# A one-core transformer trunk with a mixture of experts: new places for the gather buffers, three weight loads issued later, and a hand-written order for GpSimd's tail

## The chip, the cores and the metric

The kernel runs on one core of one Trainium2 chip. Its engines are TensorE (PE in the rows; PEld is its loading of weights), VectorE (DVE), ScalarE (ACT), GpSimd (POOL) and SyncE (SP, which here only issues DMAs). The metric is the device time of one execution in microseconds.

## The reference

```python
def reference(x, ...):
    h = x
    for l in range(DEPTH):                       # DEPTH = 1, SEQ = 1024 tokens, D_MODEL = 1024
        h = h + hybrid_mixer(rms_norm(h, norm1_g[l]), ...)      # mLSTM heads ++ gMLP groups, W_out
        h = h + hierarchical_moe(rms_norm(h, norm2_g[l]), ...)  # 32 experts, top 2
    return rms_norm(h, final_g)

def hierarchical_moe(xn, w_rg, b_rg, w_re, b_re, w_gate, w_up, w_down):
    ...                                          # a group of experts, then the top 2 of its 8 experts
    def expert_block(args):                      # 128 rows of tokens that chose expert e
        xblk, e = args
        hid = jax.nn.silu(xblk @ w_gate[e]) * (xblk @ w_up[e])      # 1024 -> 512
        return hid @ w_down[e]                                       # 512 -> 1024
    ...                                          # each row weighted and added to its token
```

## The kernel before

The first 470 us or so are the mixer, in two halves of 512 tokens. The last thing that it does (`last_out`) is the second half of the output projection, one tile of 128 tokens at a time; behind each tile stand its normalisation for the experts (`scaled`, `logits_c`, `normed`, which writes the normed tokens to `xd` in DRAM) and its routing: `route_a` (which two experts), `route_pr`, `route_so`, `route_c` (the slot of each token at its experts) and `route_d` (GpSimd scatters token and weight to the table `slots`). The products of matrices take three passes of TensorE: an operand is split by ScalarE and VectorE into a rounded part `wr` and a rest `wl` (`split`, L106 and L107), and `mm3` (L111 to L113) multiplies the parts.

Then `ranks()` orders the 32 experts by their number of tokens: matmuls over `masks`, a short chain on VectorE (`key`, `kc`, `rk`, `ohp`), the matmul of L913 and the list `perm`, from which SyncE and GpSimd read the numbers of the experts. The first three experts (NSTAT = 3) are fixed ones; their tokens' numbers come from `toki` (L873). After `ranks()` the pools of the mixer are closed and the pool `mo` is opened on their memory:

```python
    rk = ranks()
    stA.close()
    mo = ctx.enter_context(tc.tile_pool(name="mo", bufs=2, side="right"))
    xes = [mo.tile([P, D], F32, name=f"xe{i}", bufs=1) for i in range(NXE)]
```

Three tiles `xe0` to `xe2` take the gathered tokens of the next experts. `fetch` reads an expert's slots (`sx_`) and gathers its tokens from `xd` by an indirect DMA of GpSimd (L1042). For each expert, TensorE transposes the tokens (L1102, `prep`), ScalarE and VectorE split them (`split_ps`, L1048 and L1049), then come the products with gate and up (each with its weights in four chunks of 512 KB), `hid` = silu(gate) * up (L1146), its transposes (L1153, `turn`), and the product with down; the result is added to `hd` in DRAM by an indirect DMA. The transposes of `hid` of one expert stand in TensorE's order in the middle of the next expert's gate product. Experts with few tokens (64 rows or less) are multiplied without splitting, by L1056.

The weights come in chunks of 512 KB into a cycle of 35 buffers (`slot`, `wchunk`), nearly all issued by SyncE, in the order of their use. A buffer is free when its chunk has been split, or multiplied. The chunks of the first experts are loaded during the mixer (`prefetch`, `prefetch_first`); `held` are the first PD = 3 chunks of the third expert's down matrix. Before, they are issued by ScalarE at the end of `last_out`.

The order of each engine's instructions is the tile framework's own up to the second expert of the loop, but for `last_out`, where all engines keep the program's order; from the second expert on TensorE, VectorE and ScalarE keep the program's order (`by_hand`).

The tail: eight tiles of 128 finished rows come back from `hd`. `stage_a` sums the squares on ScalarE and takes the root by a pow on GpSimd (L1335); `stage_b` multiplies on VectorE (L1345) and stores (SyncE, L1346). The last expert's rows are added apart (`rows_sum`), written back to `hd` (L1358), normalised (`rows_a`, `rows_b`) and scattered to the output (L1350), after all stores. In the tail VectorE and ScalarE keep the program's order (TMS); GpSimd's is the framework's.

## Time and profile before

| | |
|---|---|
| time, median of 3 runs | 1079.59 us (1076.97 to 1082.15) |
| the profiled execution's own time | 1077.55 us |
| its span, from the first to the last instruction | 1075.8 us |
| TensorE busy | 984.6 us, 92% |
| VectorE, ScalarE, GpSimd busy | 600.1, 520.9, 207.9 us |
| mean DMA rate over the span | 262 GB/s |

All times of rows are microseconds from the start of the span. The profiled execution's own time is 1.8 us more than its span, and 2.0 us less than the median of the three runs. A tile's name in a row stands without its number; `out<-in` is what an instruction writes and reads.

### The profile page before, as it was taken

How to read it: one execution, taken by the hardware profiler on the slowest of the kernel's cores; microseconds unless marked ns; L12 is line 12 of the kernel's file. 1: busy time of each engine (PE TensorE's matmuls, PEld its weight loads, DVE VectorE, ACT ScalarE, POOL GpSimd, SP SyncE). 2: the span in 40 equal slices, each digit the busy share in tenths (PEclk: the TensorE clock that was granted, in tenths of full speed). 3: DMA queues.
4: the chain of work that ended last, by engine and by line, in shares of the span. 5: the costliest groups of instructions: out<-in, count | busy, mean ns of one | idle time of the engine just before them, and what ended most of it. 6: DMA issues, size and time to landing. Idle time of an engine off the chain costs nothing. (4 is left out here: it accounts for less than half of the span.)

```text
span 1075.8 us, 16181 instructions
## 1 busy us (share of the span) xinstructions
PE 984.6 (92%) x5489; PEld 762.7 (71%) x5489; DVE 600.1 (56%) x1234; ACT 520.9 (48%) x779; POOL 207.9 (19%) x259
## 2 busy tenths in 40 slices
PE   6999999999999999949999999999799998999960
PEld 6999887889899887737766666655566665767520
DVE  6644899656655897677834342433342455658123
ACT  6753645255534553347834433444333464758222
POOL 4310000011300000343212222321211221311123
PEclk9999999999999999979999999999899998999995
DMA  7534212444239313976999999999999999999985
GB/s 273 183 99 124 80 67 72 144 136 132 80 105 351 99 60 107 344 271 210 366 330 396 373 362 372 347 377 389 363 381 364 356 364 374 354 373 392 389 313 221
DMA packets 105460, 282.28 MB, mean 262 GB/s; under 512 B 13666, under 2 KB 40370, under 8 KB 105376
## 3 DMA queue, kind: packets, MB, share of 16 engines
q1 hardware_dynamic: 92080, 251.76, 63.8%
q0 software_dynamic: 11712, 24.75, 8.9%
q10 hardware_dynamic: 1584, 4.72, 1.2%
q8 instruction: 44, 0.72, 0.3%
q14 instruction: 40, 0.33, 0.1%
HBM read 261.62 MB, written 25.72 MB: 267 GB/s over the span
## 5 line engine op out<-in xcount | busy, mean ns | idle before, releaser
L107 DVE TENSOR_TENSOR wl<-raw,wr 128x1024 fp32r<-128x1024 f32 (+2 forms) x219 | 259.1, 1191 | 195.8 <-ACT wr L106 183.1
L106 ACT ACTIVATE wr<-raw 128x1024 fp32r<-128x1024 f32 (+2 forms) x219 | 223.6, 1028 | 229.7 <-PE acc L113 166.4
L111 PE MATMUL acc<-wr,r 128*128 128x512 f32 (+2 forms) x688 | 265.1, 386 | 1.7 <-ACT r L1048 0.9
L112 PE MATMUL acc<-wl,r 128*128 128x512 f32 (+2 forms) x688 | 260.5, 379 | 0.0
L113 PE MATMUL acc<-wr,l 128*128 128x512 f32 (+2 forms) x560 | 208.3, 375 | 0.0
L111 PEld LDWEIGHTS acc<-wr,r 128*128 128x128 f32 x688 | 130.5, 190 | 25.5 <-issue 5.1
L112 PEld LDWEIGHTS acc<-wl,r 128*128 128x128 f32 x688 | 130.8, 190 | 15.2 <-issue 0.5
L1056 PE MATMUL acc<-raw,r 128*64 128x256 f32 (+1 forms) x864 | 132.3, 453 | 2.6 <-ACT r L1083 2.4
L113 PEld LDWEIGHTS acc<-wr,l 128*128 128x128 f32 x560 | 106.2, 190 | 11.4 <-DVE l L235 0.6
L1056 PEld LDWEIGHTS acc<-raw,r 128*64 128x64 f32 x864 | 59.8, 138 | 58.8 <-issue 27.9
L111 PE MATMUL acc<-wr,xer 128*128 128x512 f32 x144 | 59.9, 416 | 0.0
L113 PE MATMUL acc<-wr,xel 128*128 128x512 f32 x144 | 57.4, 398 | 0.0
L112 PE MATMUL acc<-wl,xer 128*128 128x512 f32 x144 | 57.3, 398 | 0.0
L1102 PEld LDWEIGHTS sm<-ident,xe 64*128 64x128 f32 (+1 forms) x272 | 33.9, 197 | 31.8 <-issue 15.8
L1056 PE MATMUL acc<-raw,xer 128*64 128x256 f32 x448 | 52.9, 383 | 0.7 <-ACT xer L1083 0.7
L1102 PE MATMUL sm<-ident,xe 64*128 64x64 f32 (+1 forms) x272 | 38.8, 286 | 14.9 <-DMA xe<-xd,toki 8.6
L111 PE MATMUL acc<-r,wr 128*128 128x512 f32 x128 | 51.5, 402 | 0.0
L112 PE MATMUL acc<-l,wr 128*128 128x512 f32 x128 | 51.0, 398 | 0.0
L113 PE MATMUL acc<-wr,r 128*128 128x512 f32 x128 | 50.7, 396 | 0.0
L113 PE MATMUL acc<-r,wl 128*128 128x512 f32 x128 | 50.5, 395 | 0.0
L1056 PEld LDWEIGHTS acc<-raw,xer 128*64 128x64 f32 x448 | 30.8, 137 | 17.3 <-issue 1.0
L1083 ACT ACTIVATE r<-sm 128x256 f32<-128x256 f32 (+1 forms) x28 | 12.7, 453 | 44.4 <-PE sm L1153 44.1
(477 smaller groups left out, 1368.9 us busy)
## 6 DMA issues: line engine op xcount, KB each, us to landing
raw<-in_w_up_dram SPq DMA_DIRECT2D x119, 512.0 KB, 11.6
raw<-in_w_down_dram SPq DMA_DIRECT2D x113, 512.0 KB, 11.2
raw<-in_w_gate_dram SPq DMA_DIRECT2D x111, 512.0 KB, 11.6
raw<-in_w_in_dram SPq DMA_DIRECT2D x24, 412.0 KB, 3.5
raw<-in_w_in_dram SPq DMA_DIRECT2D x16, 512.0 KB, 3.9
raw<-in_w_out_dram SPq DMA_DIRECT2D x16, 512.0 KB, 3.6
raw<-in_w_in_dram SPq DMA_DIRECT2D x16, 410.0 KB, 4.0
l<-in_w_gate_dram SPq DMA_DIRECT2D x11, 512.0 KB, 12.8
```

What stands on the lines that cost most here:

```text
L106: nc.scalar.activation(r[:, :n], raw[:, :n], AF.Copy)
L107: nc.vector.tensor_tensor(l[:, :n], raw[:, :n], r[:, :n].bitcast(F32), op=OP.subtract)
L111: nc.tensor.matmul(ps, ar, br, start=first, stop=False)
L112: nc.tensor.matmul(ps, ar, bl, start=False, stop=False)
L113: nc.tensor.matmul(ps, al, br, start=False, stop=last)
L1056: nc.tensor.matmul(ps[q * H:(q + 1) * H, :n], x, w[:, q * n:(q + 1) * n], start=first, stop=last)
L1083: nc.scalar.activation(x, ps[0][:, :kt * H], AF.Copy)
L1102: nc.tensor.transpose(ps[-1][:, k % per * w:(k % per + 1) * w], xk_[:w, k], ident[:w, :w])
```

## The change

Four edits. The pool `mo` first makes five tiles (`spare`), so that `xe0` to `xe2` lie 16 KB further up: before, `xe0` lay on the last flips' buffers `kT` and `qT`, and `xe1` on `key` and `ohp`; after, all three lie on the mixer's `y` (and the end of `xe2` on `lga`), while the split tokens `xer` and `xel` lie where `xe0` and `xe1` did. The first gather is made at once there, and the last tile's two scatters (`route_d`) stand behind it instead of ahead of it in the text. The three chunks `held` are issued by ScalarE behind the first expert's split tokens (`pin["XE"]`). In `last_out` the last multiply of `scaled` moves from VectorE to GpSimd. In the tail GpSimd too keeps the program's order, and the write-back of the last rows becomes a step of its own, next to last.

```diff
--- before.py
+++ after.py
@@ -43,7 +43,7 @@
 LOOK = 8
 YS = (5, 7)
 E_ = mybir.EngineType
-TMS = (E_.DVE, E_.Activation)
+TMS = (E_.DVE, E_.Activation, E_.Pool)
 MS = (E_.PE, E_.DVE, E_.Activation, E_.Pool)
 NXE = 3
 RE, RL, RT = 14, 9, 3
@@ -664,8 +664,6 @@
                 with tc.issue_after(pin["POOL"].ins):
                     route_d(T // P - 2, 0)
                     route_d(T // P - 2, 1)
-                    route_d(T // P - 1, 0)
-                    route_d(T // P - 1, 1)
                 break
             if nh:
                 po = [acc() for _ in range(TT)]
@@ -782,12 +780,10 @@
             if t + 1 == TT:
                 prefetch_first()
             prefetch(XO + RE + RL + PF[t])
-        scaled(g0 + TT - 1, ys[TT - 1], 1, nc.vector)
+        scaled(g0 + TT - 1, ys[TT - 1], 1)
         raw_logits(g0 + TT - 1, 1)
         normed(TT - 1)
         prefetch(XO + RE + RL + PF[-1], eng=nc.scalar)
-        for z in sources(NSTAT - 1, 2)[:PD]:
-            held.append(wchunk(z, nc.scalar, True))
         route_d(g0 + TT - 3, 1)
         route_a(g0 + TT - 1)
         route_pr(g0 + TT - 1)
@@ -1021,11 +1017,30 @@
     rk = ranks()
     stA.close()
     mo = ctx.enter_context(tc.tile_pool(name="mo", bufs=2, side="right"))
+    spare = [mo.tile([P, KT, P], F32R, name="xe" + q, bufs=1) for q in "rl"]
+    spare += [mo.tile([P, FF], F32, name="hid", bufs=2) for _ in range(2)]
+    spare.append(mo.tile([P, D], F32, name="yo", bufs=1))
     xes = [mo.tile([P, D], F32, name=f"xe{i}", bufs=1) for i in range(NXE)]
     for a in xes[NSTAT:]:
         nc.scalar.activation(a, nhalf[:, 0:1].to_broadcast([P, D]), AF.Copy)
     slots5 = slots.rearrange("(b e) w -> b e w", e=NE)
     ngat = [0]
+
+    gathered = {}
+
+    def gather(at, n, a=None):
+        if a is None:
+            a = xes[ngat[0] % NXE]
+            ngat[0] += 1
+        pin["XG"] = nc.gpsimd.indirect_dma_start(out=a[:n], out_offset=None, in_=xd,
+                                                 in_offset=bass.IndirectOffsetOnAxis(ap=at, axis=0),
+                                                 bounds_check=T - 1, oob_is_err=False)
+        return a
+
+    gathered[0] = gather(toki[:, 0:1], P)
+    with tc.issue_after(pin["XG"].ins):
+        route_d(T // P - 1, 0)
+        route_d(T // P - 1, 1)
 
     def fetch(e, base, n, a=None):
         sx_ = mo.tile([P, 1, 4], I32, name="sx_", bufs=8)
@@ -1036,16 +1051,14 @@
             rows_ = slots5[base:base + n] if isinstance(base, int) else slots5[ds(base, n)]
             nc.gpsimd.dma_start(sx_[:n], rows_[:, ds(e, 1)])
         if a is None:
-            a = xes[ngat[0] % NXE]
-            ngat[0] += 1
-        at = toki[:n, e:e + 1] if isinstance(e, int) else sx_[:n, 0, 0:1]
-        nc.gpsimd.indirect_dma_start(out=a[:n], out_offset=None, in_=xd,
-                                     in_offset=bass.IndirectOffsetOnAxis(ap=at, axis=0),
-                                     bounds_check=T - 1, oob_is_err=False)
+            a = gathered.pop(e) if isinstance(e, int) and e in gathered else \
+                gather(toki[:n, e:e + 1] if isinstance(e, int) else sx_[:n, 0, 0:1], n)
+        else:
+            gather(sx_[:n, 0, 0:1], n, a)
         return a, sx_, n
 
     def split_ps(ps, r, l):
-        nc.scalar.activation(r, ps, AF.Copy)
+        pin["XE"] = nc.scalar.activation(r, ps, AF.Copy)
         nc.vector.tensor_tensor(l, ps, r.bitcast(F32), op=OP.subtract)
 
     H = P // 2
@@ -1265,9 +1278,12 @@
         last = i + 1 == NE
         if i == 0:
             ahead()
-            feed()
             cur = Expert(blks[r], take, pump)
             cur.prep()
+            with tc.issue_after(pin["XE"].ins):
+                for z in sources(NSTAT - 1, 2)[:PD]:
+                    held.append(wchunk(z, nc.scalar))
+            feed()
         while loads and loads[0][0] <= i + 1:
             j, e, m = loads.pop(0)
             skip[0] = (e, m) == (NE - 1, 2)
@@ -1355,6 +1371,8 @@
         for nh in range(2):
             hv, pd = slice(nh * 512, (nh + 1) * 512), prev.pd[0][nh]
             nc.vector.tensor_tensor(rows_[:n, hv], rows_[:n, hv], pd[:n], op=OP.add)
+
+    def rows_back():
         nc.gpsimd.indirect_dma_start(out=hd, out_offset=bass.IndirectOffsetOnAxis(ap=sx[:n, 0, 1:2], axis=0),
                                      in_=rows_[:n], in_offset=None, bounds_check=T + P - 1, oob_is_err=True)
 
@@ -1370,7 +1388,7 @@
             steps.append((stage_a, t))
         if t:
             steps.append((stage_b, t - 1))
-    steps.append((rows_b,))
+    steps += [(rows_back,), (rows_b,)]
     for f, at in ((rows_a, YS[1]), (rows_sum, YS[0])):
         steps.insert(at, (f,))
     with tc.manual_schedule(engines=set(TMS)):
```

**VectorE at the end of the routing.** The rows behind the token numbers `toki`; `key` to `ohp` is the ranking, `ws` to `idxs` the last tile's slots, `wl` the splits of the first expert's gate matrix. Before:

```order
L905 SCALAR_TENSOR_TENSOR key<-sm,keyr 32x32
L907 SCALAR_TENSOR_TENSOR kc<-sm,keyc 32x1
L909 TENSOR_SCALAR key<-key,kc 32x32
L910 TENSOR_REDUCE rk<-key 32x1
L912 TENSOR_SCALAR ohp<-row_304,rk 32x32
L914 CAST perm<-sm 1x32
L916 COPY cnt<-sm 48x32
L875 SCALAR_TENSOR_TENSOR ws<-d,sg 128x1
L877 RECIPROCAL pay<-ws 128x1
L878 TENSOR_TENSOR pay<-d,pay 128x1
L880 SCALAR_TENSOR_TENSOR oh,pos<-row_304,e_4835,sm 128x32 x2
L107 TENSOR_TENSOR wl<-raw,wr 128x1024
```

After:

```order
L871 SCALAR_TENSOR_TENSOR ws<-d,sg 128x1
L901 SCALAR_TENSOR_TENSOR key<-sm,keyr 32x32
L873 RECIPROCAL pay<-ws 128x1
L903 SCALAR_TENSOR_TENSOR kc<-sm,keyc 32x1
L874 TENSOR_TENSOR pay<-d,pay 128x1
L876 SCALAR_TENSOR_TENSOR oh,pos<-row_304,e_4829,sm 128x32
L905 TENSOR_SCALAR key<-key,kc 32x32
L876 SCALAR_TENSOR_TENSOR oh,pos<-row_304,e_4829,sm 128x32
L906 TENSOR_REDUCE rk<-key 32x1
L107 TENSOR_TENSOR wl<-raw,wr 128x1024
L878 SCALAR_TENSOR_TENSOR idxs<-pos,e_4829 128x2
L908 TENSOR_SCALAR ohp<-row_304,rk 32x32
```

The ranking's `ohp`, the fifth row before, is now the twelfth: ahead of it stand `ws`, the two rows of `pay`, both of `oh`, the first split (`wl`) and `idxs`, which all stood behind it. In the whole program VectorE's order differs at two more places: the multiply of `scaled` is gone, and the one shown last here.

**GpSimd from the first gather on**, with what each row waits for (PE_, DVE_, Activation_ and Pool_ are counts of an engine's instructions, DMAHW and DMASW of landed transfers). The first wait for PE is in both programs for the same count, that of the ranking's last matmul (L913 before, L909 after). Before:

```order
L1042 DMA xe_4921<-xd,toki 128x1024 [waits DMAHW2_49,DMAHW1_49,DMAHW4_49,DMASW3_49,DMAHW5_49,PE_49,DMAHW7_49,Activation_49,Pool_49]
L1042 DMA xe_4922<-xd,toki 128x1024 [waits DMASW4_49]
L1187 TENSOR_LOAD perm [waits DVE_49]
L885 DMA slots<-pay,idxs 36864x4 [waits DMASW5_49,DVE_49]
L885 DMA slots<-pay,idxs 36864x4 [waits DMASW6_49]
```

After:

```order
L1035 DMA xe_4918<-xd,toki 128x1024 [waits DMAHW2_49,DMAHW1_49,DMAHW4_49,DMASW3_49,DMAHW5_49,PE_49,DMAHW7_49,Activation_49,Pool_49]
L881 DMA slots<-pay,idxs 36864x4 [waits DMASW4_49]
L881 DMA slots<-pay,idxs 36864x4 [waits DMASW5_49]
L1035 DMA xe_4919<-xd,toki 128x1024 [waits DMASW6_49]
L1035 DMA xe_4920<-xd,toki 128x1024 [waits DMASW7_49]
```

The list of waits of the first gather is word for word the same; the two scatters of the last tile (36864x4) now stand between the first gather and the second.

**VectorE at the first expert's hidden values** (`l_5035` and `l_5040` are rests of the second expert's tokens, `wl` splits of the weights that follow). Before:

```order
L1049 TENSOR_TENSOR l_5035<-sm,r_5034 128x512 x2
L107 TENSOR_TENSOR wl<-l_4796,wr 128x1024
L107 TENSOR_TENSOR wl<-r_4798,wr 128x1024
L107 TENSOR_TENSOR wl<-raw,wr 128x1024 x2
L1146 TENSOR_TENSOR hid<-hid,acc 128x512
L107 TENSOR_TENSOR wl<-raw,wr 128x1024 x2
```

After:

```order
L1062 TENSOR_TENSOR l_5040<-sm,r_5039 128x512 x2
L1159 TENSOR_TENSOR hid<-hid,acc 128x512
L107 TENSOR_TENSOR wl<-l_4796,wr 128x1024
L107 TENSOR_TENSOR wl<-r_4798,wr 128x1024
L107 TENSOR_TENSOR wl<-raw,wr 128x1024 x4
L1062 TENSOR_TENSOR r_5115<-sm,r_5115 128x512
```

The multiply that makes `hid`, four splits later before, is now ahead of these four splits. TensorE's order is the same in both programs in every row. ScalarE's differs only in the three loads, which stood ahead of `eg` (L843) and now stand behind the two rows of `xer`. In the tail GpSimd's nine pows (L1335, now L1351) now all stand ahead of the write-back, where two stood behind it.

## Rows read from the trace of the kernel before

**Rows 1.** The page: its span, and the busy time of each engine with its share of the span and its instructions.

```profile
span 1075.8 us, 16181 instructions
...
PE 984.6 (92%) x5489; PEld 762.7 (71%) x5489; DVE 600.1 (56%) x1234; ACT 520.9 (48%) x779; POOL 207.9 (19%) x259
```

**Rows 2.** Stretches of the span: per stretch its bounds, its length, then the busy time and the instructions of PE, PEld, DVE, ACT and POOL, the granted TensorE clock, the share of the 16 DMA engines, and GB/s. The stretches are the wait at the start of the expert phase, the expert phase's second 12 us, and the rest of the expert phase.

```profile
core 0: us, PE busy (x) PEld busy (x) DVE busy (x) ACT busy (x) POOL busy (x), PEclk, DMA share, GB/s
...
472.00:488.00 16.00, 5.38 (x36) 4.29 (x36) 9.27 (x30) 5.46 (x9) 8.15 (x7) 0.50 0.88 304
...
490.00:502.00 12.00, 12.00 (x58) 9.75 (x56) 10.23 (x10) 10.89 (x12) 9.10 (x14) 1.00 0.29 85
...
514.00:1038.00 524.00, 496.74 (x2831) 336.06 (x2831) 227.67 (x235) 246.11 (x325) 113.71 (x102) 0.98 1.01 369
```

**Rows 3.** TensorE's instructions in the order of time (start, length, engine, line, operation, tiles, and the idle time before with what ended it): the ranking's last matmul, and the first transposes of the first expert's tokens.

```profile
475.62 0.18 PE L913 MATMUL sm<-ohp,ecol 32*1 32x32 bf16 x1 [1.06 <-DVE ohp L912]
484.42 1.94 PE L1102 MATMUL sm<-ident,xe 128*128 128x128 f32 x8 [8.61 <-DMA xe<-xd,toki]
```

**Rows 4.** GpSimd's instructions in the order of time, from the routing of the last tokens to the third gather.

```profile
461.90 1.31 POOL L706 TENSOR_TENSOR y<-y,g2b 128x512 f32<-128x512 f32 x1
469.03 0.57 POOL L119 TENSOR_TENSOR rs<-ms,nhalf 128x1 f32<-128x1 f32 x1 [5.82 <-DVE ms L117]
...
477.01 2.08 POOL L1042 DMA_INDIRECT xe<-xd,toki  x1 [3.66 <-ACT wr L106]
...
481.70 1.01 POOL L885 DMA_INDIRECT slots<-pay,idxs  x1 [0.31 <-DVE wl L107]
...
484.30 1.04 POOL L1042 DMA_INDIRECT xe<-xd,toki  x1 [0.30 <-issue]
```

**Rows 5.** The line of the gather, in a stretch that holds the first one alone (first row), and in one that holds the first two (the other rows): instruction, count, durations (ns, min/median/max), first and last start, and the time from issue to landing (min/median/max, us; the smallest is the first gather's, the largest the second's). POOLq is GpSimd's sequencer: the EVENT_SEMAPHORE is the last piece of the first gather's wait.

```profile
L1042 POOLq EVENT_SEMAPHORE  x1: 43/43/43, 476.2 to 476.2; - x1
...
L1042 POOL DMA_INDIRECT xe<-xd,toki x2: 1997/2040/2083, 477.0 to 479.4; - x2
...
DMA to landing us min/median/max: 7.1/8.5/10.0
```

**Rows 6.** VectorE's instructions in the order of time, from the last token tile's statistics to the first split of an expert's weights.

```profile
467.94 0.69 DVE L706 TENSOR_TENSOR y<-y,g2b 128x512 f32<-128x512 f32 x1
...
474.46 0.16 DVE L873 TENSOR_TENSOR toki<-tokc,sm 128x3 int32<-128x3 f32 x1 [1.06 <-PE sm L871]
...
475.35 0.22 DVE L912 TENSOR_SCALAR ohp<-row,rk 32x32 bf16<-32x32 bf16 x1
...
476.04 0.14 DVE L875 SCALAR_TENSOR_TENSOR ws<-d,sg 128x1 f32<-128x1 f32 x1
...
476.94 1.22 DVE L107 TENSOR_TENSOR wl<-raw,wr 128x1024 fp32r<-128x1024 f32 x1
478.08 0.15 DVE L882 SCALAR_TENSOR_TENSOR idxs<-pos,e 128x2 int32<-128x2 f32 x1
```

**Rows 7.** ScalarE's instructions in the order of time (ACTq is its sequencer, which issues DMAs): the first of three weight loads, and what stands behind them.

```profile
471.18 1.45 ACTq L989 DMA_DIRECT2D l<-in_w_down_dram  x1
...
473.67 0.30 ACT L843 ACTIVATE eg<-lga,ng 128x4 f32<-128x4 f32 x1 [2.89 <-DMA xd<-y]
...
474.06 3.88 ACT L106 ACTIVATE wr<-raw 128x1024 fp32r<-128x1024 f32 x4
```

**Rows 8.** The DMA queue of SyncE: the four loads of a gate matrix that wait for the ranking and for the first splits; and what that queue waited for in 490 to 560 us (total us, times, longest).

```profile
478.19 3.81 SPq L989 DMA_DIRECT2D raw<-in_w_gate_dram  x4
...
SPq L989 <- DVE wl L107: 41.1, 26, 9.0
```

**Rows 9.** VectorE (first two rows) and TensorE (the others) around the first expert's hidden values, in the order of time.

```profile
497.95 1.23 DVE L107 TENSOR_TENSOR wl<-l,wr 128x1024 fp32r<-128x1024 f32 x1
...
502.50 0.68 DVE L1146 TENSOR_TENSOR hid<-hid,acc 128x512 f32<-128x512 f32 x1
...
499.22 0.40 PE L111 MATMUL acc<-wr,r 128*128 128x512 f32 x1
...
503.24 0.66 PE L1153 MATMUL sm<-ident,hid 128*128 128x128 f32 x4 [1.06 <-DVE hid L1146]
```

**Rows 10.** What TensorE waited for from 484 us to the end of the expert phase: the largest entry, and the one for weights (total us, times, longest).

```profile
PE sm L1153 <- DVE hid L1146: 16.3, 12, 4.6
...
PE acc L1056 <- DMA raw<-in_w_up_dram: 0.2, 1, 0.2
```

**Rows 11.** The tail, in the order of time: GpSimd's pow of the second token tile, the write-back of the last rows (L1358) and the pow behind it; then VectorE's multiplies that overlap with them and the one that waits for the second pow.

```profile
1045.18 1.64 POOL L1335 TENSOR_TENSOR rsf<-ms,nhalf 128x1 f32<-128x1 f32 x1 [0.82 <-DVE ms L1333]
...
1055.43 1.36 POOL L1358 DMA_INDIRECT hd<-xe,sx__9235  x1 [0.33 <-DMA out_dram<-l]
1056.82 0.77 POOL L1335 TENSOR_TENSOR rsf<-ms,nhalf 128x1 f32<-128x1 f32 x1
...
1045.12 1.28 DVE L1345 SCALAR_TENSOR_TENSOR r<-raw,rsf 128x1024 f32<-128x1024 f32 x1
...
1055.89 1.28 DVE L1345 SCALAR_TENSOR_TENSOR raw<-raw,rsf 128x1024 f32<-128x1024 f32 x1
...
1057.62 1.28 DVE L1345 SCALAR_TENSOR_TENSOR raw<-raw,rsf 128x1024 f32<-128x1024 f32 x1 [0.39 <-POOL rsf L1335]
```

## The prediction

> **What bounds the kernel now.** I read the page first, for the span and the busy times [rows 1]: TensorE is busy for 92% of 1075.8 us, so an edit is worth something only where TensorE stands still, or where it delays what TensorE works on. The table of windows comes next, with one line for each stage that the diff touches [rows 2]. In 514 to 1038 TensorE is busy for 496.74 of 524 us and the DMA engines' share is 1.01: both are at their limit. In 490 to 502 TensorE is busy for all of the 12 us, the DMA engines for 0.29. In 472 to 488 TensorE works for 5.38 of 16 us; the clock granted to it averages 0.50 there.
>
> Then I read TensorE's instructions in the order of time across that hole [rows 3]: the ranking's last matmul ends at 475.62 + 0.18 = 475.80, the next instruction, the first expert's transposes, starts at 484.42, and the 8.61 us between them end with the landing of the first gather. That is the one large wait near the edits. The weights are not late behind it: for them TensorE waits 0.2 us up to the end of the phase, against 16.3 us for `hid` [rows 10]. What makes the weights come no earlier is the buffers: SyncE's queue waits 41.1 us in 490 to 560 for VectorE's splits, 26 times [rows 8]. So when the first expert starts d us later, the splits, and with them the loads behind them, come d us later too, and in the stretch behind 514 neither TensorE nor the DMA engines have the room to make it good. I carry a delay at 484 to the end at full price, and a gain too.
>
> **The gather's place.** The edit puts the buffers on other memory, but in the order of the changed program the first gather has the same list of waits, the one for the ranking's last matmul included. Before, the last piece of its wait ends at 476.2 [rows 5], 0.4 us behind that matmul's end, and the gather runs at 477.01 [rows 4]: 1.21 us from the matmul's end to the gather. I take it that this wait is the last one after the change as well, and keep the 1.21 us. What counts then is when the ranking ends.
>
> **The ranking's order on VectorE.** Before, the chain from `toki` at 474.46 reaches `ohp` at 475.35, 0.89 us later; `ws`, `pay`, `oh`, the first split and `idxs` come behind it, from 476.04 to 478.08 + 0.15 = 478.23, 2.19 us [rows 6]. The changed program puts these ahead of `ohp`. The first split does not wait for ScalarE any more: its four roundings start at 474.06, behind three issues of weight loads that begin at 471.18 with 1.45 us each and behind `eg` [rows 7], and without the issues they come earlier. So the delay of `ohp` lies between 1.22 us (the split alone, the small ones falling into the gaps of the chain) and 2.19 us (all of it back to back); half-way, +1.7.
>
> **The multiply of `scaled`.** VectorE loses 0.69 us at 467.94 [rows 6], GpSimd gains one of 1.31 us, the duration of its twin at 461.90, and it had 5.82 us of idle time at 469.03 behind it [rows 4]. The chain through `normed` to `toki` can win nothing or 0.69; GpSimd's own multiply is part of that chain and may end later than VectorE's would have. I take −0.5. Together the gather starts +1.2 later, at about 478.2.
>
> **From gather to transposes.** The first gather took 7.1 us to land, the second 10.0 [rows 5]. Its issue took 2.08 us beside VectorE's splits, a later one 1.04 [rows 4], so −1.0 is possible; on the other side the scatters now follow it on GpSimd and the four gate loads of SyncE (issued 478.19 to 482.00 [rows 8]) move with the ranking as well, which could push its latency towards the mean of the two, 8.5 us [rows 5]; half of that difference is +0.7. I take 0: transposes at 484.42 + 1.2 = 485.6.
>
> **The first `hid`.** Before, VectorE made the split at 497.95 (1.23 us), and TensorE's first chunk of the second expert's gate product started on it at 499.22; `hid` followed at 502.50, and TensorE stood still 1.06 us for it ahead of the transposes at 503.24 [rows 9]. In the changed order `hid` stands ahead of that split. It needs the end of the up product, which is when TensorE turns to the next chunk: about 499.2 in the old clock. So VectorE waits there, multiplies (0.68), then splits (1.23), and TensorE's chunk starts 0.68 + 1.23 and some 0.1 of handovers (from the split's end at 499.18 to 499.22 it was 0.04), 2.0 us later, at 501.2. The transposes of `hid` then find it ready: two chunks, 499.22 to 502.18 (503.24 less the stall) = 2.96 us less some gaps, 2.8, give 504.0 where there was 503.24. Net +0.8; for the four splits that pile up behind I take +1.0. Bounds: 0 (the old stall swapped for the new one, the splits caught up), and +2.0 (the old stall is not given back because the later splits are late in turn).
>
> **The three loads.** 3 x 512 KB leave ScalarE's queue at 471 and start behind `xer`, about 488 to 494, when the DMA engines have 0.71 of their time free in 490 to 502 [rows 2]: 0. They were due only for the third expert. If that time weren't free, 1.57 MB at 369 GB/s [rows 2] would be 4.3 us.
>
> **The second gather** moves behind two scatters (1.01 us each with 0.3 before it [rows 4]), from 479.4 [rows 5] to about 478.2 + 2.1 + 2.6 = 482.9. With 7.1 to 10.0 us it lands at 490.0 to 492.9; its transposes stand behind the first expert's up product, which now ends about 494 or later. Hidden, 0; the cover is about a microsecond in the bad case.
>
> **The tail.** The write-back at 1055.43 (1.36 us) goes behind the pows, and the pow at 1056.82 could start about 0.7 us earlier, its input being there; VectorE waited 0.39 us for it [rows 11]. But then it runs beside VectorE's multiply of 1055.89 to 1057.17. The pow of 1045.18 did just that, beside the multiply of 1045.12 to 1046.40: it took 1.64 instead of 0.77 us and ended at 1046.82, 0.4 us behind the multiply. The same here gives 1057.6, as before. So 0, with −0.4 (the wait gone) and +0.5 (the write-back now late for the last scatter) as bounds.
>
> [...]
>
> **Sum**: 1.2 + 0 + 1.0 + 0 + 0 + 0 = +2.2 us. On the profiled execution's 1077.55 us (1075.8 of span and 1.8 around it) that is 1079.75; that execution is 2.04 us under the median of the runs, so on the median I predict 1079.59 + 2.2 = 1081.8.
>
> **The rivals.**
> *The gather comes earlier.* If the wait for the ranking is not the last one, the gather waits for the token numbers and the write of the normed tokens alone. `toki` at 474.46 + 0.16 less 0.5 is 474.1, and with the same 1.21 us the gather runs at about 475.3, 1.7 us earlier than 477.01; with a quieter DMA −1.0, with `hid` +1.0: −1.7, about 1077.9. For it speaks that the text asks for the gather right behind the ranking's start of the pool; against it the list of waits, unchanged. It would still be within what can be measured.
> *The moved loads cost DMA time.* If the DMA engines are busy when the three loads come, by the gathers and gate loads that slipped, 4.3 us are added to the 2.2: 1079.59 + 6.5 = 1086.1, slower. It decides if the share in 490 to 502 rises from 0.29 to about 1 and weight waits appear on TensorE; against it, 12 us x 0.71 = 8.5 us are free for 4.3.
> *The second gather is late.* With three loads of 1.57 MB beside it, it may land at 495 or 496 instead of 493, and TensorE stands still 1 to 2 us in its transposes: 1083 to 1084.
> *Nothing of it reaches the end.* The four chunks of slip are absorbed by buffers loaded ahead, or gather and order cancel: 1079.6.
> *A real gain.* Only the hole of 8.61 us is large enough for 5.4 us; it would need a gather both 1.7 earlier and 4 us quicker. 512 KB at 369 GB/s [rows 2] are 1.4 us of the 7.1, so it isn't excluded.
>
> **How the numbers follow.** Half a per cent, 5.4 us, is about what a measurement of this kernel can tell from no change: under 1074.2 is faster, over 1085.0 slower. Chances: my forecast (1080 to 1083) 0.42; the earlier gather 0.17; nothing reaches the end 0.10; the late second gather 0.13; the costly loads 0.10; the real gain 0.08. The range leaves out the real gain and the upper part of the costly loads: 1076.5 to 1086.0; the low end is the earlier gather with its bounds. Faster 0.08; slower 0.12, the costly loads and a tail of the late gather; same 0.80.
>
> **What would show it.** Right: `ohp` behind a split, the first gather at about 478, transposes near 485.6, TensorE's hole 8 to 9 us behind a later matmul; a stall of about 2 us of TensorE for a split near 500 and none for the first `hid`; a DMA share in 490 to 502 of 0.6 or more with no wait for weights; the pow near 1056 taking about 1.6 us. Wrong: the gather before the ranking's last matmul, a landing within 5 us, TensorE waiting for weights or for the second gather near 494, or a span of the stretch behind 514 that changes by more than the slip at 510.

## The result, and the profile after

The changed kernel takes 1085.30 us (median of 5 runs, 1084.07 to 1086.86) against 1079.66 us (1076.97 to 1082.15) for the kernel before: ratio 1.0052, 95% interval [1.0031, 1.0072], 5.6 us more. The forecast was 2.2 us more. The direction held, and the median lies in the range, just under its upper end of 1086.0; the size is two and a half times the forecast's. It also lies just over the 1085.0 from which the forecast calls the kernel slower, to which it gave a chance of 0.12.

The profiled execution has a span of 1083.6 us. Its windows over the stretches of [rows 2], with the same columns:

```profile
472.00:488.00 16.00, 1.80 (x24) 1.29 (x23) 7.02 (x27) 4.27 (x7) 8.39 (x6) 0.50 0.53 184
490.00:502.00 12.00, 12.00 (x50) 9.74 (x49) 6.46 (x7) 7.96 (x10) 7.36 (x11) 0.81 0.64 212
514.00:1038.00 524.00, 496.39 (x2815) 338.00 (x2815) 230.44 (x230) 248.61 (x326) 112.08 (x101) 0.98 1.02 371
```

In 472 to 488 TensorE has 1.80 us of work where it had 5.38, at the same granted clock. In 490 to 502 the DMA share is 0.64 instead of 0.29 (2.55 MB moved instead of 1.02, of which the three loads are 1.57), and the granted clock still averages 0.81. Behind 514 nothing has changed: both limits stand as they stood.

TensorE in the order of time, to be read against [rows 3] and [rows 9]:

```profile
476.72 0.18 PE L909 MATMUL sm<-ohp,ecol 32*1 32x32 bf16 x1 [2.49 <-DVE ohp L908]
489.08 1.94 PE L1115 MATMUL sm<-ident,xe 128*128 128x128 f32 x8 [12.18 <-DMA xe<-xd,toki]
...
498.19 1.05 PE L1115 MATMUL sm<-ident,xe 128*128 128x128 f32 x8
...
506.65 0.50 PE L112 MATMUL acc<-wl,r 128*128 128x512 f32 x1 [1.68 <-DVE wl L107]
...
509.33 0.60 PE L1166 MATMUL sm<-ident,hid 128*128 128x128 f32 x4
```

The ranking's last matmul ends at 476.90 (475.80 before), but the transposes of the first expert's tokens come at 489.08 instead of 484.42: +4.66. The second transposes are at 498.19, in the trace of before at 492.83: +5.36. TensorE then stands still 1.68 us for a split, and the transposes of `hid` come at 509.33 instead of 503.24: +6.09. From there on the lag is steady for 200 us: every group of transposes from 512 to 712 us is 6.02 to 6.04 us later than its twin.

VectorE (against [rows 6] and [rows 9]):

```profile
464.38 0.69 DVE L767 TENSOR_TENSOR y<-acc,y 128x512 f32<-128x512 f32 x1
...
465.17 1.61 DVE L858 TENSOR_SCALAR so<-row,skey 128x128 bf16<-128x128 bf16 x3
...
474.13 0.16 DVE L869 TENSOR_TENSOR toki<-tokc,sm 128x3 int32<-128x3 f32 x1 [1.06 <-PE sm L867]
...
475.25 1.20 DVE L107 TENSOR_TENSOR wl<-raw,wr 128x1024 fp32r<-128x1024 f32 x1
...
476.45 0.21 DVE L908 TENSOR_SCALAR ohp<-row,rk 32x32 bf16<-32x32 bf16 x1
...
477.93 2.34 DVE L107 TENSOR_TENSOR wl<-raw,wr 128x1024 fp32r<-128x1024 f32 x2
...
504.77 0.69 DVE L1159 TENSOR_TENSOR hid<-hid,acc 128x512 f32<-128x512 f32 x1 [1.60 <-PE acc L113]
```

GpSimd (against [rows 4]), then SyncE's gate loads and ScalarE's first roundings (against [rows 7, 8]):

```profile
465.30 1.26 POOL L704 TENSOR_TENSOR y<-y,g2b 128x512 f32<-128x512 f32 x1 [2.77 <-DVE skey L853]
...
477.80 3.40 POOL L1035 DMA_INDIRECT xe<-xd,toki  x1 [4.79 <-PE sm L909]
...
484.09 1.04 POOL L1035 DMA_INDIRECT xe<-xd,toki  x1 [0.30 <-issue]
```

```profile
478.66 2.77 SPq L985 DMA_DIRECT2D raw<-in_w_gate_dram  x4
...
472.50 3.88 ACT L106 ACTIVATE wr<-raw 128x1024 fp32r<-128x1024 f32 x4
```

The first gather starts 0.79 us later than before, and its issue takes 3.40 us where it took 2.08. ScalarE's roundings start at 472.50 instead of 474.06, VectorE's first split at 475.25 instead of 476.94.

The tail, GpSimd first (against [rows 11]):

```profile
1063.71 1.97 POOL L1351 TENSOR_TENSOR rsf<-ms,nhalf 128x1 f32<-128x1 f32 x2 [1.01 <-DVE ms L1349]
...
1065.20 1.28 DVE L1361 SCALAR_TENSOR_TENSOR raw<-raw,rsf 128x1024 f32<-128x1024 f32 x1 [0.38 <-POOL rsf L1351]
```

The last two pows take 1.97 us together, and the multiply at 1065.20 waits 0.38 us for the last-but-one of them (0.39 before). From the last transposes of `hid` to the end it is 39.99 us, before 39.88.

The two profiled spans are 7.8 us apart, more than the medians. The lag is 6.03 us at 718 and 7.7 at the last `hid`; between them it goes down to 4.2 and up to 8.8 as TensorE's granted clock falls at other moments in the two executions (772 to 780 us before: 0.50 and 0.69 in windows of 4 us; 778 to 786 in the changed kernel: 0.59 and 1.00). The largest step is this one of the changed kernel (windows, columns as above), where a stall for `hid` is followed by a stretch at a granted clock of 0.50:

```profile
946.00:952.00 6.00, 2.68 (x20) 1.38 (x18) 5.03 (x5) 3.35 (x4) 0.00 (x0) 1.00 1.01 335
952.00:958.00 6.00, 5.47 (x22) 3.15 (x23) 1.16 (x2) 0.60 (x1) 0.00 (x0) 0.50 1.00 399
```

In the trace of before the granted clock is 1.00 in every 6 us window of 940 to 964. I take the 6.0 us as the change's and the rest as these two executions'; the medians (5.6) agree with that.

### The profile page after: what moved, and what is told of

Its sections match the earlier page's. It is cut to its first block, busy times and chain, and to the rows that moved or that the text cites. A ratio compares the mean times of both kernels' runs of the same rounds, so it can differ in the third digit from the quotient of the medians.

```text
span 1083.6 us, 16180 instructions
## 1 busy us (share of the span) xinstructions
PE 985.4 (91%) x5489; PEld 764.0 (71%) x5489; DVE 599.7 (55%) x1233; ACT 520.3 (48%) x779; POOL 209.5 (19%) x260
## 5 line engine op out<-in xcount | busy, mean ns | idle before, releaser
L1166 PE MATMUL sm<-ident,hid 128*128 128x128 f32 x100 | 18.3, 297 | 17.6 <-DVE hid L1159 17.6
```

What stands on the lines that cost most here:

```text
L1166: nc.tensor.transpose(ps[:, j * P:(j + 1) * P], self.hid[b][:, j * P:(j + 1) * P], ident)
```

## The experiments

Theory A: the move of the three loads causes the loss. It takes three issues out of ScalarE's queue, so ScalarE's roundings and VectorE's splits run earlier, and they disturb the gather. Rival B: GpSimd's new order and the gathers that follow closely cost it. Rival C: SyncE's gate loads, which now come ahead of the gather's packets.

Every execution reaches `toki` at another moment (472.99 to 476.81, since the mixer's length varies), so the table counts from the start of `toki`, in us, from the trace of each kernel. Ratios are against the runs of before on the same chip (medians 1078.4 to 1079.7). "To transposes" is from the end of the first gather's issue to TensorE's first transposes.

| kernel | gather starts | its issue | to transposes | transposes at | `hid` transposes at | median | ratio to before [95%] |
|---|---|---|---|---|---|---|---|
| before | 2.55 | 2.08 | 5.33 | 9.96 | 28.78 | 1079.66 | |
| after | 3.67 | 3.40 | 7.88 | 14.94 | 35.20 | 1085.30 | 1.0052 [1.0031, 1.0072] |
| loads_back | 2.25 | 1.05 | 6.06 | 9.36 | 28.03 | 1076.95 | 0.9989 [0.9973, 1.0005] |
| loads_alone | 8.53 | 1.06 | 5.84 | 15.42 | 35.81 | 1085.66 | 1.0068 [1.0053, 1.0082] |
| ohp_first | 2.58 | 4.53 | 6.73 | 13.84 | 34.20 | 1082.82 | 1.0040 [1.0024, 1.0056] |
| gate_loads_late | 3.67 | 3.39 | 3.49 | 10.55 | 29.67 | 1081.26 | 1.0027 [1.0014, 1.0040] |
| rank_off | 1.11 | 2.15 | 3.65 | 6.91 | 28.47 | 1077.12 | 0.9980 [0.9970, 0.9990] |
| rank_off_loads_back | 1.06 | 1.06 | 4.45 | 6.56 | 26.54 | 1076.91 | 0.9981 [0.9968, 0.9995] |
| rank_off_splits_late | 1.06 | 1.05 | 3.53 | 5.64 | 33.82 | 1085.42 | 1.0053 [1.0032, 1.0074] |
| hid_last | 3.67 | 3.40 | 7.60 | 14.66 | 34.50 | 1085.31 | 1.0050 [1.0032, 1.0069] |
| two_gathers_first | 1.11 | 1.05 | 3.67 | 5.83 | 31.96 | 1082.64 | 1.0049 [1.0031, 1.0066] |
| rank_off_loads_back_gates_late | 1.05 | 1.05 | 5.07 | 7.17 | 26.61 | 1075.07 | 0.9959 [0.9943, 0.9975] |
| tail_alone | 2.56 | 2.09 | 4.76 | 9.41 | 28.04 | 1079.84 | 1.0007 [0.9995, 1.0020] |
| splits_behind_issue | 1.06 | 1.06 | 3.72 | 5.84 | 25.89 | 1075.62 | 0.9975 [0.9962, 0.9988] |

**The loads' move undone, and the loads' move alone.** loads_back, on the changed kernel:

```diff
+        for z in sources(NSTAT - 1, 2)[:PD]:             # in last_out
+            held.append(wchunk(z, nc.scalar, True))
-            with tc.issue_after(pin["XE"].ins):          # behind the first expert's split tokens
-                for z in sources(NSTAT - 1, 2)[:PD]:
-                    held.append(wchunk(z, nc.scalar))
```

> The changed kernel with one edit undone: the three loads `held` are issued by ScalarE in `last_out` again. Theory A (the loads' move is the cause: without the three issues ScalarE's roundings come early, VectorE's first split gets ahead of `ohp`, the first gather starts and is issued later, and the gate loads of SyncE get ahead of its packets): VectorE's order of before comes back, the first gather starts at 476 to 477, its transposes at 483.5 to 485 (changed kernel 489.08), TensorE's stall of 1.7 us for a split goes and that for `hid` of about 1 us comes back; time 1079 to 1080.5. Rival B (the gather's new place costs it: the two scatters and the next gathers follow it closely, and the other edits of the routing): the transposes stay at 488 to 489 and the time at 1084 to 1086.

VectorE's order of before comes back with that edit alone, at `ohp` and at `hid`. GpSimd, VectorE and TensorE of loads_back:

```profile
479.06 1.05 POOL L1037 DMA_INDIRECT xe<-xd,toki  x1 [3.37 <-DMA l<-in_w_down_dram]
...
479.31 1.22 DVE L107 TENSOR_TENSOR wl<-raw,wr 128x1024 fp32r<-128x1024 f32 x1
...
486.17 1.94 PE L1117 MATMUL sm<-ident,xe 128*128 128x128 f32 x8 [8.01 <-DMA xe<-xd,toki]
```

The gather is issued just before the first split and takes 1.05 us. The transposes, expected at 483.5 to 485, come at 486.17, because `toki` came 2.68 us later in this execution than in the changed kernel's; counted from `toki` they are at 9.36 us, where the kernel before has 9.96. The time is back at that of before. loads_alone is the reverse, the last edit of the diff put on the kernel before:

> The kernel before with one edit of the four alone: the three loads `held` behind `xer`. Theory A: all of the loss comes with it: transposes at 488 to 489.5, first expert's `hid` transposes about 6 us later than the 503.24 of before, time 1084.5 to 1086. Rival B: less than 2.5 us of loss, transposes at 485 to 486, time 1080 to 1082.

It costs 7.3 us by the medians, all of the change's loss; whether it is more can't be told, as the two intervals overlap. GpSimd and VectorE:

```profile
478.16 4.30 POOL L883 DMA_INDIRECT slots<-pay,idxs  x1 [3.79 <-DVE ohp L910]
...
484.02 1.06 POOL L1040 DMA_INDIRECT xe<-xd,toki  x1 [0.30 <-issue]
...
479.28 2.34 DVE L107 TENSOR_TENSOR wl<-raw,wr 128x1024 fp32r<-128x1024 f32 x2
```

Here the last tile's scatters still stand ahead of the gather in the text, and VectorE's early split lets the first of them go ahead. Its issue takes 4.30 us, beside splits that end at 479.28 + 2.34 = 481.62; the gather is issued 5.9 us after it. So theory A holds, and rival B is out: with the gather in its old place the same loss comes, through a scatter that is held up ahead of the gather.

**`ohp` ahead of the splits.**

```diff
-        nc.vector.tensor_scalar(oh, ioe[:NE], rk, None, op0=OP.is_equal)
+        pin["OHP"] = nc.vector.tensor_scalar(oh, ioe[:NE], rk, None, op0=OP.is_equal)
-                st.enter_context(tc.issue_after(pin["TOK"].ins))
+                st.enter_context(tc.issue_after(pin["OHP"].ins))
```

> The changed kernel with VectorE's first splits held behind `ohp` (an order on one engine, no wait). If the split ahead of `ohp` is what counts, with the ranking's delay of 1.1 us and the long issue behind it: gather at 476.6, transposes at 485 to 487, time 1081 to 1083.5. If the gather's landing is set by the gate loads alone, which come earlier by the same amount: transposes 1.1 us earlier, 488.0, time 1084.

```profile
477.86 3.47 DVE L107 TENSOR_TENSOR wl<-raw,wr 128x1024 fp32r<-128x1024 f32 x3
...
477.74 4.53 POOL L1035 DMA_INDIRECT xe<-xd,toki  x1 [3.70 <-ACT wr L106]
```

The gather starts 1.09 us earlier, as it should, but its issue now takes 4.53 us and ends at the same distance from `toki` (7.11 and 7.07): 0.94 us behind the last split (477.86 + 3.47 = 481.33). Waiting for the ranking and waiting for the splits lie side by side. The transposes come 1.1 us earlier, the number of the second alternative, though the issue's length shows that its reason (the gate loads alone) isn't the whole of it; the median, 1082.82, lies in the range of the first.

**The gate loads behind the gather.**

```diff
+    pin["PR"] = nc.sync.dma_start(rt.tile([1, 1], F32, name="probe"), gathered[0][:1, :1])
-            feed()
+            with tc.issue_after(pin["PR"].ins):
+                feed()
```

> The changed kernel with SyncE's four gate loads behind the landing of the first gather (a load of 4 bytes from the gathered tokens stands ahead of them in SyncE's queue). If the 2 MB of gate loads that are issued ahead of the gather's packets cost it 2.5 us or more: the gather lands within 5 us of the end of its issue (7.8 in the changed kernel, 5.0 before), transposes at 485 to 486.5, time 1081.5 to 1083, unless the gate loads are then missed (TensorE waiting for weights near 520). If the latency comes from the scatters and gathers of GpSimd's own queue: transposes at 488 to 489, time as the changed kernel or worse.

```profile
479.55 3.39 POOL L1035 DMA_INDIRECT xe<-xd,toki  x1 [4.78 <-PE sm L909]
...
486.44 1.95 PE L1116 MATMUL sm<-ident,xe 128*128 128x128 f32 x8 [7.79 <-DMA xe<-xd,toki]
...
488.09 3.73 SPq L985 DMA_DIRECT2D raw<-in_w_gate_dram  x4
```

Start and issue of the gather are those of the changed kernel to 0.01 us, and from the end of the issue to the transposes it is 3.49 us instead of 7.88. So 4.4 us of the latency come with the 2 MB of gate loads. The four further kernels in which the three loads are late and no gate load is issued ahead of the end of the gather's issue agree: 3.53 to 3.72 us in the table. Rival C is no rival but the second half of the mechanism: in the changed kernel the issue, 477.80 to 481.20, is held up so long that all four loads (the last at 481.10) are issued before it ends. The ratio to before falls from 1.0052 to 1.0027, less than the 5.5 us by which `hid` is earlier; from the last `hid` to the end it is 41.49 us here, 39.99 in the changed kernel.

**The gather off the ranking.**

```diff
-        key = lp[0].tile([NE, NE], F32, name="key")
+        key = rt.tile([NE, NE], F32, name="key")
-        oh = lp[0].tile([NE, NE], BF16, name="ohp")
+        oh = rt.tile([NE, NE], BF16, name="ohp")
```

> The changed kernel with the ranking's `key` and `ohp` in the pool `rt`, so that the first gather waits for `toki` instead of the ranking's last matmul; VectorE's order is the changed kernel's, with the first split 1.1 us behind `toki`. If the gather's issue on GpSimd is held up by VectorE's splits (3.4 us in the changed kernel, 1.0 without): the gather starts 1 to 1.3 us behind `toki` (3.67 in the changed kernel) at the same moment as the first split; if it is first it takes 1.0 us and lands within 6 us, transposes 7 to 8 us behind `toki` (14.95 in the changed kernel); if the split is first, its issue takes 4 to 5.5 us and nearly nothing is won, transposes 13 to 15 us behind `toki`. If instead the wait for the ranking is what costs, transposes 2.5 us earlier with an issue of 3.4 us: 12.4 us behind `toki`.

```profile
475.78 2.15 POOL L1035 DMA_INDIRECT xe<-xd,toki  x1 [2.22 <-DVE oh L876]
...
481.58 1.94 PE L1115 MATMUL sm<-ident,xe 128*128 128x128 f32 x8 [4.13 <-DMA xe<-xd,toki]
...
491.89 1.16 PE L1115 MATMUL sm<-ident,xe 128*128 128x128 f32 x8 [1.55 <-DMA xe<-xd,toki]
```

With these two tiles outside the closed pools, the first gather no longer waits for the ranking: it runs at 475.78, the ranking's last matmul at 477.27. It starts together with the first split (475.79), takes 2.15 us, and the transposes come 8.0 us earlier than in the changed kernel. The second transposes now wait 1.55 us for the second gather, which is why only 6.7 us reach `hid`. The issue lies between the cases that I had written down (1.0 us, 4 to 5.5 us), and the transposes, 6.91 us behind `toki`, just below the better one (7 to 8). The kernel beats the one before by 0.2%.

With the loads back as well:

> The changed kernel with `key` and `ohp` in `rt` and the three loads in `last_out` again: the gather waits for `toki` alone and VectorE's splits come late. Theory: gather 1.0 to 1.3 us behind `toki`, issue 1.0 us, in front of all gate loads, transposes 6 to 7.5 us behind `toki` (9.96 in the kernel before, 9.36 with the loads back alone): 2 to 3 us less than with the loads back alone, time 1074 to 1075.5. Rival (the landing is set by the three loads, still in the DMA engines until 478): transposes 8.5 to 9.5 us behind `toki`, time 1076 to 1077.5.

The transposes are as the theory said (6.56), the time of 1076.91 as the rival said: against the kernel before 2.24 us are won at `hid` (26.54), and by the medians 2.0 us. The second gather and the first split of this run:

```profile
478.74 1.01 POOL L1037 DMA_INDIRECT xe<-xd,toki  x1 [0.30 <-issue]
...
478.82 1.22 DVE L107 TENSOR_TENSOR wl<-raw,wr 128x1024 fp32r<-128x1024 f32 x1
```

This issue began 0.08 us ahead of a split and ran beside it in the usual 1.01 us, so here a split doesn't slow an issue that is under way. What the runs of splits delay in the other kernels would then be its beginning.

**The splits behind the ranking.** As rank_off, and `pin["CNT"]` (the copy of `cnt`) in place of `pin["TOK"]`:

> The changed kernel with `key` and `ohp` in `rt` and VectorE's first splits behind the ranking's last instruction (`cnt`), the three loads late as in the changed kernel. Theory (what costs is that the splits come ahead of the gather's issue and let the gate loads go first): gather 1.0 to 1.3 us behind `toki`, issue 1.0 us, transposes 6 to 7 us behind `toki`, `hid` with its 0.7 us loss; time 1074.5 to 1076.5. Rival (the moved loads cost by themselves, in the DMA engines behind 490): transposes early, but TensorE waits later for weights or the second gather, time 1078 to 1082.

```profile
478.59 4.61 DVE L107 TENSOR_TENSOR wl<-raw,wr 128x1024 fp32r<-128x1024 f32 x4
...
477.72 1.05 POOL L1035 DMA_INDIRECT xe<-xd,toki  x1 [2.19 <-DVE key L905]
479.08 5.01 POOL L881 DMA_INDIRECT slots<-pay,idxs  x1 [0.30 <-issue]
...
485.67 1.04 POOL L1035 DMA_INDIRECT xe<-xd,toki  x1 [0.30 <-issue]
...
493.52 0.48 PE L1115 MATMUL sm<-ident,xe 128*128 128x128 f32 x1 [8.17 <-DMA xe<-xd,toki]
```

The first gather is free of everything, transposes 5.64 us behind `toki`, and the kernel is as slow as the changed one. The scatter behind the gather is now beside four splits in a row, its issue takes 5.01 us, the second gather starts at 485.67, and TensorE waits 8.17 us for it. The theory's time was missed by 9 us, the rival's by 3. The rival's symptom came (a late second gather), its reason (the moved loads' own DMA time) did not.

**The order at `hid`.**

```diff
-        nc.vector.tensor_tensor(l[:, :n], raw[:, :n], r[:, :n].bitcast(F32), op=OP.subtract)
+        pin["SPL"] = nc.vector.tensor_tensor(l[:, :n], raw[:, :n], r[:, :n].bitcast(F32), op=OP.subtract)
-                    nc.vector.tensor_tensor(h, h, ps[b], op=OP.mult)
+                    with tc.issue_after(pin["SPL"].ins):
+                        nc.vector.tensor_tensor(h, h, ps[b], op=OP.mult)
```

> The changed kernel with the multiply that makes the first `hid` behind the splits emitted ahead of it, as in the kernel before. From the first expert's second transposes to the transposes of `hid` the kernel before takes 10.41 us, the changed one 11.14. If the order on VectorE is the cause: 10.4 again, TensorE's stall for the split (1.7 us) gone and one for `hid` of about 1 us back, time 0.7 below the changed kernel. If the later splits are late anyway: 11.1 and no difference.

```profile
499.19 1.05 PE L1115 MATMUL sm<-ident,xe 128*128 128x128 f32 x8
...
509.60 0.66 PE L1167 MATMUL sm<-ident,hid 128*128 128x128 f32 x4 [1.06 <-DVE hid L1160]
```

509.60 - 499.19 = 10.41 us, the number of before, against 11.14 in the changed kernel; the 1.06 us wait for `hid` is back. The 0.73 us are this order's: it is 10.41 us also in loads_back and tail_alone, where `hid` stands behind the splits, and 11.14 and 11.15 in ohp_first and loads_alone, where it stands ahead. The median doesn't show them (1085.31), its interval is 4 us wide.

**Two gathers first.** As rank_off_splits_late with hid_last, and `gathered[0]` and `gathered[1]` both issued ahead of the scatters:

> The changed kernel (three loads late) with `key` and `ohp` in `rt`, VectorE's first splits behind `cnt`, the first `hid` behind the splits, and the second gather ahead of the last tile's two scatters. In the kernel with the splits late the second gather stood behind a scatter whose issue took 5.01 us beside the splits, and TensorE stood still 8.2 us for it. Theory: the second gather's issue is over before the splits (1.0 us each), transposes of the first expert 5.6 us behind `toki`, no wait for the second gather, `hid` transposes 24.5 to 26 us behind `toki` (28.78 in the kernel before, 26.54 with ranking off and loads back), time 1074 to 1076. Rival: the loss that the late loads bring is of another kind (their own DMA time), then TensorE waits for the second gather or for weights again and `hid` comes at 28 us or more, 1078 or more. Rival for the end: what is won at the start is given back by the loads, which are at the DMA engines' limit behind 514 us; then the time stays at 1076 to 1077 with an earlier `hid`.

```profile
475.41 1.05 POOL L1035 DMA_INDIRECT xe<-xd,toki  x1 [2.23 <-DVE oh L876]
476.76 4.95 POOL L1035 DMA_INDIRECT xe<-xd,toki  x1 [0.30 <-issue]
...
476.21 4.61 DVE L107 TENSOR_TENSOR wl<-raw,wr 128x1024 fp32r<-128x1024 f32 x4
...
488.90 1.12 PE L1116 MATMUL sm<-ident,xe 128*128 128x128 f32 x4 [5.72 <-DMA xe<-xd,toki]
```

The theory failed: splits start at 476.21, the second issue at 476.76, and it takes 4.95 us, until 0.9 us behind the last split (480.82). TensorE waits 5.72 us.

**Splits behind the issue.** The same, but the splits wait until both gathers are issued:

```diff
+    flag = rt.tile([P, 2], F32, name="flag")
+    with tc.issue_after(pin["XG"].ins):
+        pin["FL"] = nc.gpsimd.memset(flag[:, 0:1], 0.0)
+    pin["CNT"] = nc.vector.tensor_copy(flag[:, 1:2], flag[:, 0:1])
```

> As the kernel with two gathers first, but VectorE's first splits wait until GpSimd has issued both gathers (GpSimd clears a word behind the second issue, VectorE copies it ahead of the splits). If VectorE's run of splits is what holds up the issue: both issues take 1.0 to 1.1 us (the second took 4.95), TensorE's wait of 5.7 us for the second gather goes, the first expert's transposes come 5.5 to 6.5 us behind `toki` and the transposes of `hid` 25 to 26.5 us behind it (31.96 with two gathers first, 28.78 in the kernel before); time 1073.5 to 1076. If the second gather's issue is long for another reason (its wait, the scatters, the DMA queue): it takes 4 us or more again, TensorE waits for it 4 us or more, `hid` at 30 us or more behind `toki`, and the time stays at 1081 to 1084.

```profile
474.05 1.06 POOL L1035 DMA_INDIRECT xe<-xd,toki  x1 [2.17 <-DVE key L905]
475.41 1.01 POOL L1035 DMA_INDIRECT xe<-xd,toki  x1 [0.30 <-issue]
...
476.64 2.35 DVE L107 TENSOR_TENSOR wl<-raw,wr 128x1024 fp32r<-128x1024 f32 x2
...
481.67 1.06 PE L1120 MATMUL sm<-ident,xe 128*128 128x128 f32 x4
```

Both issues take a microsecond, TensorE's wait for the second gather is gone (no idle time ahead of the transposes at 481.67), `hid` is 25.89 us behind `toki`. Beside the start of the splits only a cleared and a copied word, and the scatters behind them, differ from two_gathers_first, so it is the run of splits that holds up the issue. ScalarE's roundings, the other work that moved forward, are not it: in the changed kernel they end at 472.50 + 3.88 = 476.38, ahead of the issue of 477.80 that took 3.40 us. The ratio goes from 1.0049 to 0.9975 with this one edit. 1075.62 us is 3.6 us less than the kernel before, with the three loads as late as in the change.

**The gate loads again, without the other faults.** rank_off_loads_back with the probe of gate_loads_late:

> As the kernel with the ranking off the gather's wait and the three loads back in `last_out`, but with SyncE's four gate loads behind the landing of the first gather. If the gate loads still cost the gather something: transposes 5.4 to 6 us behind `toki` instead of 6.56 and `hid` 25.5 to 26, but the four loads start 4 us later, and the time stays within 1 us of 1076.9. If nothing is left to win there: 6.5 us again.

Transposes at 7.17, later and not earlier: here, where the issue is free, holding the gate loads back wins nothing. Why it is 0.6 us later isn't settled. The time, 1075.07, is the lowest measured, but its interval overlaps with that of rank_off_loads_back.

**The tail alone.**

> The kernel before with the tail's edit alone (GpSimd in the program's order, the write-back of the last rows behind the pows). Prediction: the pow of the last tile but one starts about 0.7 us earlier, but beside VectorE's multiply, takes 1.4 to 1.6 us and ends where it ended before; the multiply that waits for it waits 0.4 us again, and from the last `hid` transposes to the end it is 39 to 40 us as before; ratio 1.000 within 0.0015. Rival: the wait of 0.39 us goes, and 0.4 us are gained from the multiply to the end.

```profile
1060.33 1.28 DVE L1345 SCALAR_TENSOR_TENSOR raw<-raw,rsf 128x1024 f32<-128x1024 f32 x1 [0.38 <-POOL rsf L1335]
```

The prediction's picture: the multiply's wait is 0.38 us where it was 0.39, the last `hid` to the end is 39.92 us (39.88), the ratio is not told apart from 1.

## Why the prediction was right, and where it was too small

**The wait list, and the ranking's order: right.** The gather still waits for the ranking's last matmul, and the splits ahead of `ohp` delay that. From `toki` to `ohp` it was 0.89 us and is 2.32: +1.43, forecast +1.7. From the matmul's end to the gather it is 0.90 us instead of the 1.21 that I kept.

**The multiply of `scaled`: wrong in sign.** I took -0.5, with 0 as the worst. From VectorE's last addition (`y<-acc,y`) to `toki` it is 9.75 us (474.13 - 464.38), and 9.40 in the trace of before: +0.35. VectorE is rid of 0.69 us, but its three `so` at 465.17 now run beside GpSimd's multiply of 465.30 and take 1.61 us. The price stood in the trace of before, which I read for durations only, not for what ran beside them (GpSimd, then VectorE):

```profile
456.68 1.27 POOL L706 TENSOR_TENSOR y<-y,g2b 128x512 f32<-128x512 f32 x1 [1.66 <-DVE skey L857]
...
456.54 1.62 DVE L862 TENSOR_SCALAR so<-row,skey 128x128 bf16<-128x128 bf16 x3
...
465.06 0.69 DVE L769 TENSOR_TENSOR y<-acc,y 128x512 f32<-128x512 f32 x1
...
465.85 0.58 DVE L862 TENSOR_SCALAR so<-row,skey 128x128 bf16<-128x128 bf16 x3
```

Beside GpSimd's multiply at 456.68 three `so` took 1.62 us, without one, at 465.85, 0.58. I had reckoned with such a pair in the tail only [rows 11].

**From gather to transposes: the step that failed.** I took 0, with -1.0 and +0.7 as bounds; it is +3.87 (4.66 less the 0.79 of the later start). 1.32 of it is the issue, beside splits that now run without a break: in the changed kernel they end at 477.93 + 2.34 = 480.27 and the issue at 481.20. 2.55 is the landing, since SyncE's four gate loads were issued meanwhile. I had both in hand, the 2.08 against 1.04 us of issue and the gate loads that "move with the ranking as well", and let them cancel as a -1.0 and a +0.7. What the step left out is that the gather moved back while the splits, which I had coming earlier myself, moved forward: the gather then starts inside the run of splits, and its held-up issue lets the gate loads pass. Of the signs that I had named for a right forecast, the transposes near 485.6 and a hole of 8 to 9 us did not come: it is 489.08, behind a hole of 12.18 us.

**The clock: not in the sum.** From the first to the second transposes it took 8.41 us and takes 9.11, as TensorE works longer at a granted clock of 0.50. Before, it is granted 0.50 from the first transposes up to 488 us, 0.82 in the next microsecond and 1.00 from 489; after, 0.50 up to 494, 0.72 in the next and 1.00 from 495. TensorE's matmuls (128x512, 0.63 us each and then 0.39) grow shorter 4.0 us behind the first transposes before, 5.4 us after. This goes with the hole ahead of them. Behind holes of 7.8 to 8.6 us (before, loads_back, tail_alone, gate_loads_late) the way to the second transposes takes 8.0 to 8.4 us, behind holes of 11.9 to 12.7 us (after, loads_alone, ohp_first, hid_last) 9.1 to 9.4 us. So the 0.70 us belongs to the late gather too, one execution of each kernel being all that says so. A longer hole isn't all there is to it: behind holes of 4 to 6 us the matmuls grew shorter after 4.1 to 6.3 us (after 12 and 14 in the two kernels where TensorE stood still in between), and why is open.

**`hid`: right.** +0.73, forecast +1.0; the stall of 1.68 us for the split came as described, and the one of 1.06 went.

Together: 0.35 + 1.43 - 0.31 + 1.32 + 2.55 + 0.70 + 0.73 = 6.77, less 0.68 by which this execution's mixer was earlier (464.38 against 465.06), is the 6.09 of the trace.

**The loads and the tail: 0, as forecast.** No wait for weights appears, and the second transposes had no wait either: the second gather, at 484.09, was in time. That the three loads cost nothing in DMA time doesn't make their move free; it was the costliest edit, through ScalarE's queue.

**Carried to the end: right** to 0.02 us from 512 to 712 us; behind that the two executions' clocks hide it, and it rests on the medians. From the last `hid` to the end, 39.1 to 42.7 us in the kernels above, a part of what some of them won early seems to be given back; that wasn't settled.

**The range: luck in part.** Its upper end was there for the moved loads' DMA time and for a late second gather, and neither came. The first gather, for which the sum allowed +0.7 us at most, filled that room instead.

## What to carry to other kernels

Taking DMA issues out of an engine's queue moved what stood behind them earlier (ScalarE's roundings from 474.06 to 472.50 us here, with `toki` 0.33 us earlier), and the scheduler let another engine follow (VectorE's first split from 476.94 to 475.25): look at what the newly early work runs beside, above all GpSimd's indirect DMAs, whose issues took 3.39 to 5.01 us here beside runs of splits and 0.95 to 1.06 without. A delay of an issue can also cost the transfer its place ahead of others: with four gate loads issued meanwhile the first gather's transposes came 7.88 us behind the end of its issue, with those loads held back (gate_loads_late) 3.49. So ask which transfers pass meanwhile, and price the latency with them ahead. For a gather on the critical path, freeing its issue (the splits wait behind it), together with taking it off the ranking's wait, made the late loads harmless: 3.6 us under the kernel before instead of 5.6 over it.

## What the runs showed of the hardware

Runs of VectorE's splits (128x1024, 1.2 us each, back to back) held up the issue of an indirect DMA on GpSimd until the run was over: issues of 3.39 to 5.01 us in eight kernels (after, loads_alone, ohp_first, gate_loads_late, hid_last, rank_off with its first scatter, rank_off_splits_late, two_gathers_first), against 0.95 to 1.06 us without splits. They ended 0.84 to 0.94 us behind the last split (for gate_loads_late and hid_last that distance isn't on record). Of the issue it seems to be the beginning that is held up: issues that began 0.08 and 0.09 us ahead of a split (rank_off_loads_back, rank_off_loads_back_gates_late) took 1.01 us beside it, but one that began only 0.01 us ahead (rank_off) took 2.15. Which part of an issue is stopped these runs don't show.

Not every run held the issue to its end. Some got in at a border between two splits and took 1.74 to 2.15 us. Before, `idxs` ended at 478.23 and the gather's issue at 479.09, in the middle of the run; the second gather there (2.00 us) and a scatter in splits_behind_issue (2.02 us) got in with nothing between the splits. In loads_alone two short instructions between splits (`perm` and `cnt`, 479.16 to 479.28) did not let the scatter in. What decides at a border is open. One thing goes with it: the splits take 1.20 to 1.21 us each in after, loads_alone, ohp_first, rank_off and hid_last, where an issue was held up to the end of the run, and 1.22 in before, loads_back, tail_alone, rank_off_loads_back and rank_off_loads_back_gates_late, where none was held up past the next border; whether that is a cause or only a sign of it isn't shown.
